# A gated hybrid layer: six of its products done as seven half-sized block products each, in a stage of their own

## The chip, the cores and the metric

The kernel runs on one core of one Trainium2 chip. The metric is the time of one execution on the device in microseconds (us); the times are medians of several runs. The profile is one more execution, taken by the hardware profiler, and its span runs from the first instruction to the last. The engines are TensorE (PE, with its weight loads as PEld), VectorE (DVE), ScalarE (ACT), GpSimd (POOL) and SyncE (SP), which here only issues DMAs.

## What is computed

One decoder layer on 2048 tokens of 1024 features, behind 16 learned meta tokens. One wide input projection feeds two branches: attention with a sliding window of 128 tokens (16 heads, 4 key heads), and a matrix memory (mLSTM, 4 heads) that runs over chunks of 64 tokens. Each branch is gated and projected, the two are merged by sigmoid gates, and there is an output projection with a norm and a residual behind it. Cut to what matters here:

```python
u = rmsnorm(h, norm_pre)
(a_q, a_k, a_v, a_z, m_qk, m_v, m_i, m_f, m_o, m_z, g_a, g_m) = split(u @ w_in)
att = swa_sink_branch(rope(a_q), rope(a_k), a_v)
y_a = (att * silu(a_z)) @ w_attn_out
cell = mlstm_cell(silu(conv(m_qk)), m_v, m_i, m_f)
hm = head_layernorm(sigmoid(m_o) * cell)
y_m = (hm * silu(m_z)) @ w_mlstm_out
merged = sigmoid(g_a) * y_a + sigmoid(g_m) * y_m
out = h + rmsnorm(merged @ w_out, norm_post)
```

Six products in it have 2048 by 1024 results and 1024 terms: a_z, m_z, g_m (columns of w_in) and the three with w_attn_out, w_mlstm_out and w_out. In the kernel they are called az, mz, gm, att, hm and out.

## The kernel before

All products are in float32 accuracy from three matmuls: each operand is split into a rounded part (hi) and the rest (lo), and hi by hi, lo by hi and hi by lo are added in PSUM. ScalarE casts hi, VectorE subtracts for lo. A result tile of 128 by 512 takes 8 blocks of 128 terms, 24 matmuls.

The main stage goes through the tokens in two halves of 1024. In each half it follows a plan of blocks (`PLAN`): four groups, each of an attention block A (q, k, v of 4 heads, `token_proj`), a feature block F (one tile each of q and k, two of ga, `feat_proj`), an mLSTM block M (v and o of one head) and a second feature block (two tiles each of az and mz); at the end of the half two feature blocks with gm. `load_w` (line 163) loads and splits the weights of each block ahead of it. `evict_f` (line 721) writes gates to DRAM.

What attention and the mLSTM do per 128 tokens is written as generators (`attn_block`, line 397, `mlstm_chain`, line 563). `slot()` (line 262) is called after every 6 projection matmuls and lets each generator that is due go on by one step; an attention block is started every 12 slots (`ATT_SLOTS`). So their matmuls stand between projection matmuls, and VectorE, ScalarE and GpSimd do the steps between. At an attention block of the plan `drain()` (line 763) has all queued attention blocks started before the next eight come. Results go to DRAM (`att_d`, `hm_d`). Each mLSTM block of 128 tokens loads a row of maxima, `mrep`, by an SP DMA (line 550).

The last stage takes 512 tokens at a time: it loads att_d and the gate az, multiplies and splits, projects (line 929), the same for hm and mz, merges, and then does the output projection (line 951) with norm and residual.

The order of TensorE's instructions is that of the code. On the other engines, and for the DMAs on SP, a scheduler sets the order by priority when the program is built; on the chip each of them takes its instructions strictly in that order.

## Time and profile before

| | us |
|---|---|
| median of 3 runs | 2421.65 |
| lowest, highest | 2418.39, 2426.34 |
| the profiled execution | 2425.9 |
| its span | 2424.2 |

The span is made of engine times, so a row of it is read as: how long an engine was busy in it, and what ended its idle time. "Releaser" is the instruction behind whose end a waiting one could start. Matmuls overlap, so the start of one to the start of the next tells what one costs, not its duration.

### The profile page before, as it was taken

Reading aid. Unit: us, or ns where it says so; the run is one execution under the profiler, and the core shown is the slowest. Engines: PE = TensorE matmul, PEld = TensorE weight load, DVE = VectorE, ACT = ScalarE, POOL = GpSimd, SP = SyncE. Lnnn points to the kernel's source line nnn. Section 1 sums busy time; section 2 is a strip of 40 time slices with the busy share of each in tenths; the row PEclk is TensorE's granted clock in tenths of the full one; section 3 lists DMA queues with packets and bytes.
Section 4 is the critical chain, followed back from the end, with each engine's and each line's share of the span. In section 5 each row is a group of like instructions: output and inputs, shape, how many; then the busy total and the mean of one; then the engine's idle time right before and its main releaser. Section 6 shows DMA issues by size and latency. Waiting matters only on the chain.

```text
span 2424.2 us, 34730 instructions
## 1 busy us (share of the span) xinstructions
PE 2377.3 (98%) x11725; PEld 2017.7 (83%) x11725; DVE 1404.7 (58%) x3309; ACT 1014.7 (42%) x2674; POOL 558.6 (23%) x1151
## 2 busy tenths in 40 slices
...
GB/s 188 51 49 96 92 56 67 70 101 44 97 56 56 89 103 143 48 59 70 90 58 63 72 47 65 74 86 58 70 85 237 230 191 254 175 254 168 236 176 89
DMA packets 176162, 261.38 MB, mean 108 GB/s; under 512 B 18684, under 2 KB 68176, under 8 KB 175984
## 3 DMA queue, kind: packets, MB, share of 16 engines
q1 hardware_dynamic: 175984, 259.17, 33.7%
...
HBM read 200.35 MB, written 58.76 MB: 107 GB/s over the span
## 4 chain that ended last, share of the span: by engine, by line
PE 82%; DMA 6%; DVE 6%; ACT 3%; issue 2%; POOL 1%; SPq 0%; DVEq 0%; POOLq 0%; ACTq 0%
PE pj L714 35%; PE pj L702 22%; PE pj L929 10%; PE pj L951 3%; PE acc L479 3%; DMA wraw<-in_w 3%; PE s L427 3%; DVE wlo L182 2%; PE acc L546 2%; ACT whi L181 1%; PE tr L452 1%; DMA xs<-att_d 1%; DMA zl<-mz_d 1%; PE tr L400 1%; PE tr L546 1%
## 5 line engine op out<-in xcount | busy, mean ns | idle before, releaser
L714 PE MATMUL pj<-un,whi 128*128 128x512 f32 x2560 | 805.1, 396 | 0.0
L702 PE MATMUL pj<-whi,un 128*128 128x512 f32 (+2 forms) x1952 | 604.1, 371 | 0.0
L714 PEld LDWEIGHTS pj<-un,whi 128*128 128x128 f32 x2560 | 467.3, 188 | 88.4
L714 PE MATMUL pj<-un,wlo 128*128 128x512 f32 x1280 | 501.8, 392 | 0.0
L182 DVE TENSOR_TENSOR wlo<-wraw,whi 128x512 fp32r<-128x512 f32 (+2 forms) x480 | 325.5, 702 | 175.4 <-ACT whi L181 172.5
L702 PEld LDWEIGHTS pj<-whi,un 128*128 128x128 f32 x1952 | 361.3, 188 | 37.7 <-issue 1.3
L181 ACT CAST whi<-wraw 128x512 fp32r<-128x512 f32 (+2 forms) x480 | 283.0, 606 | 229.1 <-DMA wraw<-in_w 135.1
L702 PE MATMUL pj<-wlo,un 128*128 128x512 f32 (+2 forms) x976 | 355.9, 365 | 0.0
L929 PE MATMUL pj<-un,whi 128*128 128x512 f32 x1024 | 315.6, 389 | 5.4 <-DVE part L934 5.2
L714 PEld LDWEIGHTS pj<-un,wlo 128*128 128x128 f32 x1280 | 240.8, 188 | 53.3
L929 PEld LDWEIGHTS pj<-un,whi 128*128 128x128 f32 x1024 | 191.9, 188 | 46.6 <-issue 3.2
L929 PE MATMUL pj<-un,wlo 128*128 128x512 f32 x512 | 199.2, 389 | 0.0
L702 PEld LDWEIGHTS pj<-wlo,un 128*128 128x128 f32 x976 | 184.1, 189 | 14.7
L951 PE MATMUL pj<-whi,un 128*128 128x512 f32 x512 | 164.3, 400 | 8.8 <-DVE y L967 8.2
L727 ACT ACTIVATE xs<-pj 128x512 f32<-128x512 f32 x128 | 76.5, 598 | 209.6 <-PE pj L714 200.2
L436 ACT ACTIVATE P<-s,mn 128x144 f32<-128x144 f32 x256 | 95.1, 376 | 152.5 <-DVE mn L434 150.5
L966 POOL TENSOR_TENSOR yss<-yss,mhalf 128x1 f32<-128x1 f32 x16 | 8.8, 549 | 621.3 <-DVE yss L965 621.3
L445 POOL TENSOR_TENSOR Pm<-P,mn 128x64 f32<-128x64 f32 x64 | 38.0, 594 | 443.8 <-DVE mn L441 351.4
L951 PEld LDWEIGHTS pj<-whi,un 128*128 128x128 f32 x512 | 98.8, 193 | 32.0 <-DVE y L967 9.4
L462 POOL TENSOR_SCALAR_AFFINE_SELECT pp<-pc 128x512 fp32r<-128x512 f32 x120 | 84.5, 704 | 175.7 <-ACT pc L457 164.0
L929 PEld LDWEIGHTS pj<-un,wlo 128*128 128x128 f32 x512 | 96.1, 188 | 20.1
L951 PE MATMUL pj<-wlo,un 128*128 128x512 f32 x256 | 101.8, 398 | 0.5 <-DVE wlo L182 0.5
...
## 6 DMA issues: line engine op xcount, KB each, us to landing
wraw<-in_w_all SPq DMA_DIRECT2D x224, 256.0 KB, 3.3
wraw<-in_w SPq DMA_DIRECT2D x192, 256.0 KB, 3.4
...
```

The lines of the kernel that those rows point to most:

```text
L181: S.copy(hi[:, :w], raw[:, :w])
L182: tt(lo[:, :w], raw[:, :w], f(hi)[:, :w], ALU.subtract)
L427: T.matmul(sp[:, pa, c0:272], lhsT=qs[:, pr, pa, :], rhs=ks[:, i, c0:272], start=(i == 0), stop=(i == 1))
L436: S.activation(P[:, 2 * pa + pr], sp[:, pa, 128:272], AF.Exp, bias=mn[:, 2 * pr + pa:2 * pr + pa + 1], scale=-1.0, accum_out=mn[:, 4 + 2 * ...
L462: G.affine_select(pp[:, i], f(pc)[:, i], pattern=[[0, 4], [-1, 128]], compare_op=ALU.is_gt, fill=0.0, base=0, channel_multiplier=1)
L479: T.matmul(acc, lhsT=l, rhs=r.rearrange("p s q -> p (s q)"), start=(i == 0), stop=(i == len(ops) - 1))
L546: T.matmul(out, lhsT=l[:, a], rhs=r[:, b_], start=(start and n == 0), stop=(stop and n == 2))
L702: T.matmul(ps[:, :w], lhsT=us[k][:, a, o:o + 128], rhs=ww[k][:, :w], start=(n == 0), stop=(n == 3 * KT - 1))
L714: T.matmul(ps, lhsT=ww[k][:, 128 * i:128 * i + 128], rhs=us[k][:, a], start=(n == 0), stop=(n == 3 * KT - 1))
L727: S.activation(th, ps, AF.Tanh, scale=0.5)
L929: T.matmul(ps, lhsT=ww[k][:, 128 * i:128 * i + 128], rhs=us[k][:, a], start=(n == 0), stop=(n == 3 * KT - 1))
L951: T.matmul(ps, lhsT=mg[k][:, a, 128 * i:128 * i + 128], rhs=ww[k], start=(n == 0), stop=(n == 3 * KT - 1))
```

## The change

az, mz and gm leave the main stage. They and the three projections with output weights become 12 sets: each matrix for each half of the tokens, a product of 1024 by 1024 by 1024. Both operands are cut in four blocks of 512 by 512, and the product is made of seven block products instead of eight, by sums and differences of blocks (`PRODS`: P1 to P7). A block product is 48 matmuls of 128 by 512, accumulated in four PSUM banks; some are added upon the bank that another left.

The blocks' sums are made where the operands come from. For weights: copies of a block of 1 MB from DRAM to DRAM on SP, and accumulating DMAs on GpSimd (`weight_sums`), a step of them at each block of the plan. For the tokens: the scaled tiles are stored to DRAM in several places (`tokens`) and three sums and more are made by accumulating DMAs (`token_sums`). For the gated att and hm and for the merged sum: on VectorE, as the results come (`operands`).

The plan now has A, F with q and k alone (256 columns), M, and after every second M an F with four tiles of ga. In the place of `drain()` there is a loop that runs slots while too many attention blocks are queued or unfinished. All memory of the main stage is given back ahead of the new stage, which has pools of its own: raw loads in 4 buffers, split operands in 4, one resident operand per product.

```diff
-        fblock([("ga", i), ("q", i), ("k", i), ("ga", i + 4)])
+        fblock([("q", i), ("k", i)])
         th(i)
-        if i < 3:
-            fblock([("az", 2 * i), ("az", 2 * i + 1), ("mz", 2 * i), ("mz", 2 * i + 1)])
-    fblock([("az", 6), ("az", 7), ("mz", 6), ("mz", 7)])
-    fblock([("gm", i) for i in range(4)])
-    fblock([("gm", i) for i in range(4, 8)])
+        if i % 2:
+            fblock([("ga", 2 * i - 2 + j) for j in range(4)])
     return plan
 
 
 PLAN = _plan()
+MATS = ("az", "mz", "gm", "att", "hm", "out")
...
+    es1 = ExitStack()
+    mconst = pool("mconst", 1, None, es1)
+    units = pool("units", 16, None, es1)
...
+    part_d = dram.tile([KT, 128, SEQ], F32, name="part_d")
+    uo_d = [[dram.tile([128, 4, SB], F32, name=f"uo{c}{i}_d") for i in range(8)] for c in range(SEQ // (2 * SB))]
+    gate_d = {n: dram.tile([KT, 128, SEQ], F32, name=f"{n}_d") for n in ("ga", "gm")}
+    sw_d = [[dram.tile([128, 4 * SB], F32, name=f"sw{m}{i}_d") for i in range(4)] for m in range(len(MATS))]
+    op_d = {(n, c): [dram.tile([128, 4, SB], F32, name=f"op_{n}{c}{i}_d") for i in range(7)]
+            for n in ("att", "hm", "mg") for c in range(SEQ // (2 * SB))}
+
+    def token_sums(c):
+        b00, b10, t2, t1, t3, b11, t4, n01 = uo_d[c]
+
+        def add(dst, src):
+            G.dma_start(out=dst, in_=src, accum_op=ALU.add, max_dma_last_dim=4096)
+
+        add(t1, n01)
+        add(t3, n01)
+        add(t2, b00)
+        yield
+        add(t2, n01)
+        yield
+        add(t4, t2)
+        yield
+
+    def weight_sums():
+        for a in range(0, len(MATS), 2):
+            pair = (a, a + 1)
+
+            def cp(dst, src):
+                nc.sync.dma_start(out=dst, in_=src)
+
+            def add(dst, src):
+                G.dma_start(out=dst, in_=src, accum_op=ALU.add, max_dma_last_dim=4096)
+
+            for m in pair:
+                cp(sw_d[m][2], wq[m, 0, 0])
+                cp(sw_d[m][0], wq[m, 1, 1])
+            yield
+            for m in pair:
+                add(sw_d[m][2], wq[m, 0, 1])
+                add(sw_d[m][0], wq[m, 0, 1])
+            yield
+            for m in pair:
+                cp(sw_d[m][1], sw_d[m][2])
+            yield
+            for m in pair:
+                add(sw_d[m][1], wq[m, 1, 1])
+            yield
+            for m in pair:
+                cp(sw_d[m][3], sw_d[m][1])
+            yield
+            for m in pair:
+                add(sw_d[m][3], wq[m, 1, 0])
+            yield
...
+                c_, s_ = divmod(t0 // SB, 2)
+                for i in ((0, 3), (5, 4, 2))[s_] if s_ == k // 4 else (() if s_ else (1,)):
+                    nc.sync.dma_start(out=uo_d[c_][i][:, k % 4], in_=xs)
+                if s_ != k // 4:
+                    neg = stage.tile([128, SB], F32, name="xs")
+                    S.activation(neg, xs, AF.Copy, scale=-1.0)
+                    nc.sync.dma_start(out=uo_d[c_][7 if s_ else 6][:, k % 4], in_=neg)
...
-                if kind == "A":
-                    drain()
+                if c or pi > 1:
+                    next(sums, None)
+                if pi in (4, 6, 8):
+                    if pi == 4:
+                        usums = token_sums(c)
+                    next(usums)
...
+                        while len(queue) > HALF_BLOCKS - 1 - i or done[0] < total - HALF_BLOCKS + i:
+                            slot()
...
-    p2 = pool("p2", 2)
...
-            for nb_ in range(2):
-                wh, wl = load_w(w2, (2 * ph + nb_) * D * SB, SB, p2)
-                for i in range(4):
-                    j = nb_ * 4 + i
-                    th = p2.tile([128, SB], F32, name="tl", bufs=3)
-                    nc.sync.dma_start(out=th, in_=gate_d[gn][j, :, sl])
-                    ps = ps_p.tile([128, SB], F32, name="pj")
-                    n = 0
-                    for k in range(KT):
-                        for a, ww in ((0, wh), (1, wh), (0, wl)):
-                            T.matmul(ps, lhsT=ww[k][:, 128 * i:128 * i + 128], rhs=us[k][:, a],
-                                     start=(n == 0), stop=(n == 3 * KT - 1))
-                            n += 1
...
+    PRODS = (("P1", 0, "w00", "b00"), ("P2", 1, "w10", "b10"), ("P6", 0, "s2", "t2"), ("P5", 1, "s1", "t1"),
+             ("P7", 0, "s3", "t3"), ("P3", 1, "s4", "b11"), ("P4", 0, "w11", "t4"))
+    NP = len(PRODS)
+    NPAIR = SEQ // (2 * SB)
+    post = pool("post", 1)
+    res = pool("res", 1)
+    ring = pool("ring", 1)
+    ps_1 = pool("ps_1", 4, PSUM)
+    ps_0 = pool("ps_0", 4, PSUM)
+    SETS = [(n, c, ("u", c)) for c in range(NPAIR) for n in ("az", "mz", "gm")]
+    SETS += [(n, c, ("w", n)) for n in ("att", "hm", "out") for c in range(NPAIR)]
+    OPD = {"att": "att", "hm": "hm", "out": "mg"}
+    IDX = {"P1": 0, "P2": 1, "P6": 2, "P5": 3, "P7": 4, "P3": 5, "P4": 6}
+
+    def split(pl, nm, src, p, sign=1.0, bufs=None):
+        raw = src.pop(0)
+        op = pl.tile([128, 2, 2, SB], R, name=nm, **({} if bufs is None else {"bufs": bufs}))
+        if sign == 1.0:
+            S.copy(op[:, 0], raw)
+            tt(op[:, 1], raw, f(op)[:, 0], ALU.subtract)
+        else:
+            S.activation(op[:, 0], raw, AF.Copy, scale=sign)
+            stt(op[:, 1], raw, sign, f(op)[:, 0], ALU.mult, ALU.subtract)
+        return op
...
+    N = len(SETS) * NP
+    fetched, ready, resident = {}, {}, {}
+
+    def fetch(n):
+        u, i = divmod(n, NP)
+        nm, c, key = SETS[u]
+        w_src = weight_src(nm, PRODS[i][2])
+        b_src = (uo_d[c] if key[0] == "u" else op_d[OPD[nm], c])[i]
+        srcs = [w_src, b_src] if key[0] == "u" else [b_src, w_src]
+        if u and SETS[u - 1][2] == key:
+            srcs.pop()
+        fetched[n] = []
+        for src in srcs:
+            for p in range(2):
+                raw = ring.tile([128, 2, SB], F32, name="raw", bufs=4)
+                nc.sync.dma_start(out=raw, in_=src[:, 2 * p:2 * p + 2])
+                fetched[n].append(raw)
+
+    def prep(n):
+        u, i = divmod(n, NP)
+        raws = fetched.pop(n)
+        st = [split(ring, "st", raws, p, bufs=4) for p in range(2)]
+        if raws:
+            sign = -1.0 if SETS[u][2][0] == "u" and PRODS[i][0] == "P6" else 1.0
+            resident[i] = [split(res, f"r{i}{p}", raws, p, sign) for p in range(2)]
+        ready[n] = (st, resident[i])
...
+    def operands(on, c, nh, sh, g, b):
+        d = op_d[on, c]
+        if (nh, sh) == (0, 0):
+            store(d[IDX["P1"]][:, g], b)
+        elif (nh, sh) == (1, 1):
+            store(d[IDX["P3"]][:, g], b)
+        elif (nh, sh) == (0, 1):
+            b11, b22 = keep[0, g], keep[1, g]
+            tt(b11, b11, b, ALU.subtract)
+            store(d[IDX["P5"]][:, g], b11)
+            tt(b, b22, b, ALU.subtract)
+            store(d[IDX["P7"]][:, g], b)
+            stt(b22, b11, -1.0, b22, ALU.mult, ALU.subtract)
+            store(d[IDX["P6"]][:, g], b22)
+        else:
+            store(d[IDX["P2"]][:, g], b)
+            t2 = keep[1, g]
+            stt(t2, t2, -1.0, b, ALU.mult, ALU.subtract)
+            store(d[IDX["P4"]][:, g], t2)
...
+        if e is not None:
+            tt(e, bank, e, ALU.add)
+        v = bank if e is None else e
+        if nm == "gm":
+            th = post.tile([128, SB], F32, name="th", bufs=2)
+            S.activation(th, v, AF.Tanh, scale=-0.5 if nh else 0.5)
+            store(gate_d["gm"][j, :, sl], th)
+        elif nm in ("az", "mz"):
+            a = ld((att_d if nm == "az" else hm_d)[j, :, sl])
+            th = post.tile([128, SB], F32, name="th", bufs=2)
+            S.activation(th, v, AF.Tanh, scale=0.5)
+            stt(th, th, -1.0 if nh else 1.0, v, ALU.add, ALU.mult)
+            b = kept(nh, sh, g)
+            if nm == "az":
+                tt(b, a, th, ALU.mult)
+            else:
+                stt(b, a, hn_t[:, j:j + 1], th, ALU.mult, ALU.mult)
+            operands("att" if nm == "az" else "hm", c, nh, sh, g, b)
+        elif nm == "att":
+            th = ld(gate_d["ga"][j, :, sl])
+            b = post.tile([128, SB], F32, name="bt", bufs=2)
+            stt(b, th, 1.0, v, ALU.add, ALU.mult)
+            store(part_d[j, :, sl], b)
...
+    with tc.high_priority(offset=300):
+        for n in range(2):
+            fetch(n)
+        prep(0)
+    for n in range(N):
+        u, i = divmod(n, NP)
+        nm, c, key = SETS[u]
+        name, bset = PRODS[i][0], (PRODS[i][1] + u) % 2
+        if n + 2 < N:
+            fetch(n + 2)
+        if n + 1 < N:
+            with (tc.high_priority(offset=200) if n == 0 else ExitStack()):
+                prep(n + 1)
+        fresh = name in ("P1", "P2", "P5")
+        if name in ("P1", "P2"):
+            banks[bset] = [(ps_1 if bset else ps_0).tile([128, SB], F32, name="x") for _ in range(4)]
+        st, rs_ = ready.pop(n)
+        ow, ob = (st, rs_) if key[0] == "u" else (rs_, st)
+        order_ = [(p, g, kk) for p in range(2) for g in range(4) for kk in range(2)]
+        if n == N - 1:
+            order_ = [(p, g, kk) for g in range(4) for p in range(2) for kk in range(2)]
+        for p, g, kk in order_:
+            for m, (a, b) in enumerate(((0, 0), (0, 1), (1, 0))):
+                if nm == "out":
+                    l, r = ob[p][:, a, kk, 128 * g:128 * g + 128], ow[p][:, b, kk]
+                else:
+                    l, r = ow[p][:, a, kk, 128 * g:128 * g + 128], ob[p][:, b, kk]
+                T.matmul(banks[bset][g], lhsT=l, rhs=r, start=(fresh and p == 0 and kk == 0 and m == 0),
+                         stop=(p == 1 and kk == 1 and m == 2), skip_group_check=True)
+        for g in range(4):
+            bk = banks[bset][g]
+            if name == "P1":
+                e1[g] = etile()
+                S.copy(e1[g], bk)
+            elif name == "P2":
+                quarter(nm, c, 0, 0, g, bk, e1[g])
+            elif name == "P6":
+                e2[g] = etile()
+                S.copy(e2[g], bk)
+            elif name == "P5":
+                e5[g] = etile()
+                S.copy(e5[g], bk)
+            elif name == "P7":
+                quarter(nm, c, 1, 1, g, bk, e5[g])
+            elif name == "P3":
+                quarter(nm, c, 0, 1, g, bk, e2[g])
+            else:
+                quarter(nm, c, 1, 0, g, bk, None)
```

The order of instructions shows it at three places. The names: `sw11` is the second of four weight sums of the second matrix, `in_wq` the weights, `mrep` the row of maxima for an mLSTM block, `wraw` a weight tile, `att_d` and `hm_d` the stores of results; in brackets stand the semaphores that a row waits for, DMASW for an accumulating DMA of GpSimd, DMAHW for a DMA of SP.

SP, in the first mLSTM block of the plan, before:

```order
L550 DMA mrep_1591<-mr_d_102 128x128 [waits DMAHW4_49,DVE_49,Activation_49]
L550 DMA mrep_1702<-mr_d_102 128x128 [waits DMAHW4_49,DVE_49,Activation_49]
L611 DMA hm_d_104<-tho_1475 128x2x128 [waits DMAHW6_49,Activation_49]
L550 DMA mrep_1819<-mr_d_102 128x128 [waits DMAHW5_49,DMAHW7_49,DVE_49,Activation_49]
L486 DMA att_d_103<-ao_1736 128x2x128 [waits DMAHW0_49,DVE_49]
L611 DMA hm_d_104<-tho_1573 128x2x128 [waits DMAHW1_49,Activation_49]
L550 DMA mrep_1896<-mr_d_102 128x128 [waits DMAHW2_49,DMAHW7_49,DVE_49,Activation_49]
L611 DMA hm_d_104<-tho_1679 128x2x128 [waits DMAHW3_49,Activation_49]
L550 DMA mrep_2007<-mr_d_102 128x128 [waits DMAHW2_49,DVE_49,Activation_49]
```

and after:

```order
L185 DMA sw11_d_132<-sw12_d_133 16x16384 [waits DMAHW2_49,DMASW6_49]
L604 DMA mrep_1425<-mr_d_105 128x128 [waits DMAHW7_49,DVE_49,Activation_49]
L226 DMA wraw2_2184<-in_w_all 128x384 [waits DMAHW4_49]
L185 DMA sw03_d_130<-sw01_d_128 16x16384 [waits DMAHW5_49,DMASW0_49]
L604 DMA mrep_1540<-mr_d_105 128x128 [waits DMAHW3_49,DMAHW6_49,DVE_49,Activation_49]
L185 DMA sw20_d_135<-in_wq 16x16384
L539 DMA att_d_106<-ao_1462 128x2x128 [waits DMAHW0_49,DVE_49]
L185 DMA sw13_d_134<-sw11_d_132 16x16384 [waits DMAHW1_49,DMASW3_49]
L185 DMA sw32_d_141<-in_wq 16x16384 [waits DMAHW2_49]
L604 DMA mrep_1617<-mr_d_105 128x128 [waits DMAHW6_49,DVE_49,Activation_49]
L185 DMA sw30_d_139<-in_wq 16x16384 [waits DMAHW4_49]
```

Between the loads of mrep there are now copies of weight blocks, three of which wait for accumulating DMAs. A little later on SP, at the last weight tiles (`wraw`) of the second attention block, after:

```order
L185 DMA sw41_d_144<-sw42_d_145 16x16384 [waits DMAHW6_49,DMASW3_49]
L665 DMA hm_d_107<-tho_1805 128x2x128 [waits DMAHW7_49,Activation_49]
L226 DMA wraw_2190<-in_w_all 128x384 [waits DMAHW0_49,DVE_49]
L604 DMA mrep_3280<-mr_d_105 128x128 [waits DMAHW4_49,DVE_49,Activation_49]
L185 DMA sw51_d_148<-sw52_d_149 16x16384 [waits DMAHW2_49,DMASW7_49]
L539 DMA att_d_106<-ao_2067 128x2x128 [waits DMAHW3_49,DVE_49]
L226 DMA wraw_2196<-in_w_all 128x384
```

Ahead of each of the two tiles there is now a copy that waits for an accumulation. GpSimd, in the first block of q and k, before (`raw` and `halo` are the convolution's borders, `Pm` and `pmb` probabilities of the meta tokens):

```order
L513 MEMSET rawm 128x38
L502 COPY halo_121<-raw 128x3
L498 COPY raw<-halo_125 128x3
L502 COPY halo_125<-raw 128x3
L498 COPY raw<-halo_121 128x3
L445 TENSOR_TENSOR Pm<-P,mn 128x64
L465 AFFINE_SELECT pc<-pc 128x512 x2
L471 TENSOR_TENSOR pmb<-pm,bm 128x512
```

and after (L169 and L188 are accumulating DMAs, of token tiles and of weights):

```order
L169 DMA uo_d<-uo_d 256x1024
L556 COPY halo_209<-raw 128x3
L463 CAST ks<-km_193 128x2x16
L188 DMA sw_d<-in_wq 256x1024
L552 COPY raw<-halo_205 128x3
L169 DMA uo_d<-uo_d 256x1024
L556 COPY halo_205<-raw 128x3
L188 DMA sw_d<-in_wq 256x1024
L498 TENSOR_TENSOR Pm<-P,mn 128x64
L552 COPY raw<-halo_209 128x3
L188 DMA sw_d<-in_wq 256x1024
L556 COPY halo_209<-raw 128x3
```

Accumulating DMAs now stand between the convolution's steps. TensorE at the end of the main stage, before (L714 the last gm tile, L929 the last stage):

```order
L714 MATMUL pj<-un,whi 128x512 x2
L714 MATMUL pj<-un,wlo 128x512
L929 MATMUL pj<-un,whi_19756 128x512 x2
L929 MATMUL pj<-un,wlo_19757 128x512
L929 MATMUL pj<-un,whi_19762 128x512 x2
```

and after (L779 the last ga tile, L453 to L532 the steps of attention blocks, L1156 the new stage):

```order
L480 MATMUL s<-ks,qs 128x272 x4
L532 MATMUL acc<-pmb,vm_200 128x512
L532 MATMUL acc<-pc,vt 128x512 x2
L532 MATMUL acc<-pp,vt 128x512 x2
L480 MATMUL s<-ks,qs 128x272 x4
L505 MATMUL tr<-ident,P 128x128 x4
L507 MATMUL acc<-ident,Pm 64x128
L532 MATMUL acc<-pmb,vm_200 128x512
L532 MATMUL acc<-pc,vt 128x512 x2
L532 MATMUL acc<-pp,vt 128x512 x2
L1156 MATMUL x<-r_16838,st 128x512 x24
L1156 MATMUL x<-r_16841,st 128x512 x24
```

Steps of attention blocks that stood between projections now stand between the last projection and the new stage.

## Rows read from the trace of the kernel before

**Rows 1.** The page, part 1: busy us, share of the span, instructions of each engine.

```profile
PE 2377.3 (98%) x11725; PEld 2017.7 (83%) x11725; DVE 1404.7 (58%) x3309; ACT 1014.7 (42%) x2674; POOL 558.6 (23%) x1151
```

**Rows 2.** Timeline of TensorE: start us, us, engine, line, operation, tiles, count.

```profile
1800.05 0.61 PE L714 MATMUL pj<-un,whi 128*128 128x512 f32 x2
...
1838.81 0.62 PE L714 MATMUL pj<-un,whi 128*128 128x512 f32 x2
...
1872.12 0.62 PE L929 MATMUL pj<-un,whi 128*128 128x512 f32 x2
```

**Rows 3.** Groups by line: count | busy us, mean ns of one | idle before, releasers.

```profile
L714 PE MATMUL pj<-un,whi 128*128 128x512 f32 x2560 | 805.1, 396 | 0.0
...
L182 DVE TENSOR_TENSOR wlo<-wraw,whi 128x512 fp32r<-128x512 f32 (+2 forms) x480 | 325.5, 702 | 175.4 <-ACT whi L181 172.5
...
L436 ACT ACTIVATE P<-s,mn 128x144 f32<-128x144 f32 x256 | 95.1, 376 | 152.5 <-DVE mn L434 150.5 <-PE tr L323 2.0
...
L462 POOL TENSOR_SCALAR_AFFINE_SELECT pp<-pc 128x512 fp32r<-128x512 f32 x120 | 84.5, 704 | 175.7 <-ACT pc L457 164.0 <-DVE pc L458 9.1 <-PE pj L714 0.2
L465 POOL TENSOR_SCALAR_AFFINE_SELECT pc<-pc 128x512 fp32r<-128x512 f32 x128 | 83.8, 677 | 5.9 <-DVE pc L458 5.9
...
L471 POOL TENSOR_TENSOR pmb<-pm,bm 128x512 fp32r<-128x512 f32 x64 | 73.5, 1149 | 0.0
L490 DVE SCALAR_TENSOR_TENSOR xs<-raw,cw,xs 128x512 f32<-128x512 f32 x96 | 71.9, 749 | 28.7 <-ACT xs L501 17.7 <-POOL halo L502 10.4
L433 DVE TENSOR_REDUCE mn<-s 128x2 f32<-128x288 f32 x128 | 58.1, 454 | 2.5
L429 DVE COPY_PREDICATED s<-um,s 128x256 f32<-128x256 int32 x120 | 50.8, 423 | 51.6 <-PE s L427 51.4
...
L447 DVE TENSOR_TENSOR P<-P,mn 128x512 f32<-128x512 f32 x64 | 46.1, 721 | 4.2 <-POOL Pm L445 1.4
...
L457 ACT CAST pc<-tr 128x512 fp32r<-128x512 f32 x64 | 37.5, 587 | 31.6 <-PE tr L452 29.5 <-POOL ropb L252 1.8
```

**Rows 4.** Waits of TensorE in the whole span, the longest total.

```profile
PE tr L609 <- DVE ks L409: 9.4, 8, 1.5
```

**Rows 5.** Stretches: length; busy PE, PEld, DVE, ACT, POOL; PEclk, DMA share, GB/s.

```profile
1116.00:1170.00 54.00, 54.00 (x262) 45.01 (x262) 31.45 (x83) 21.36 (x66) 12.51 (x22) 1.00 0.25 81
1170.00:1205.00 35.00, 35.00 (x203) 34.69 (x203) 8.43 (x20) 9.99 (x33) 13.13 (x33) 1.00 0.19 59
1205.00:1256.00 51.00, 51.00 (x244) 42.34 (x243) 33.55 (x71) 25.58 (x65) 14.88 (x27) 1.00 0.22 74
1256.00:1319.00 63.00, 62.54 (x339) 52.96 (x337) 45.41 (x138) 32.97 (x102) 22.94 (x52) 1.00 0.19 55
1730.00:1872.00 142.00, 142.00 (x651) 117.74 (x651) 53.73 (x115) 44.04 (x103) 14.71 (x22) 1.00 0.43 144
1872.00:2418.00 546.00, 531.33 (x2306) 435.69 (x2304) 320.03 (x518) 184.23 (x337) 8.23 (x15) 0.99 0.63 199
59.00:155.00 96.00, 93.53 (x467) 76.75 (x466) 71.39 (x199) 48.82 (x135) 30.38 (x55) 0.98 0.17 52
...
40.00:60.00 20.00, 13.87 (x77) 12.76 (x76) 11.55 (x26) 11.19 (x31) 12.21 (x28) 0.83 0.51 163
```

**Rows 6.** Timeline at the end: TensorE's last matmul.

```profile
2417.74 0.39 PE L951 MATMUL pj<-whi,un 128*128 128x512 f32 x1
```

**Rows 7.** Waits of SP in the whole span: us in total, times, longest.

```profile
SPq L550 <- DVE dw L576: 206.8, 59, 7.4
```

**Rows 8.** DMA queue: packets, MB, share of 16 engines; issue: KB each, us to landing.

```profile
q1 hardware_dynamic: 175984, 259.17, 33.7%
...
xr<-in_x SPq DMA_DIRECT2D x16, 512.0 KB, 4.9
```

224 lines of the change are left out of this document (112 added, 112 removed).

## The prediction, made before the changed kernel ran

> **What bounds the kernel now.** The page comes first: TensorE is busy 98% of the span, VectorE 58%, ScalarE 42%, GpSimd 23% [rows 1]. A busy TensorE need not be a fast one, so the second view is the timeline of its matmuls: in a stretch that waits for nothing, 171 projection matmuls of 512 columns start in 38.76 us (1800.05 to 1838.81), 0.227 us each [rows 2]; the 396 ns of their group are durations that overlap [rows 3]. Third, the waits: the longest total of TensorE at any one line is 9.4 us [rows 4]. Its own stream of instructions is the bound. Fourth, the busy times by stretch [rows 5], which show what the average hides. A group of four blocks runs from 1116 to 1319: az and mz (to 1170), an attention block (to 1205), q, k and ga (to 1256), an mLSTM block. VectorE is busy 58%, 24%, 66% and 72% in them, and 38% in the gm blocks (1730 to 1872). In the last stage (1872 to 2418) TensorE shows 531 of 546 us.
>
> **What is removed.** By the code a tile of 128 by 512 results takes 24 matmuls, and az, mz, gm and each output projection have 32 tiles: 6 by 768 = 4608, half of them in the main stage, half in the last (where the row counts 2306 in all [rows 5]). Afterwards 12 sets of 7 products of 48 matmuls, 4032, stand in one stage. 576 fewer by 0.227 us is 131 us off the bound, 5.4% of the span. I make the sum by stage. The main stage ends at 1872.1; without its 2304 matmuls (522 us) it would end at 1350. The new last stage is at least 4032 by 0.227, 914 us. After the last matmul some 6 us remain, from 2417.74 to the span's end [rows 6]. 1350 + 914 + 6 = 2270 us, if nothing new waited. The present last stage takes 546 us for 522 of matmuls; these 24 us of stalls are not in the floor and return below.
>
> **The block sums.** This is the largest term. The order shows 24 copies of 1 MB on SP and 29 accumulating DMAs of 1 MB on GpSimd in the first half. The code spreads them over the plan, but they stand nearly in one stretch: from the loads of the first q, k block to those of the second attention block, between the mrep loads that each mLSTM block waits for. SP and GpSimd take their rows in order; that an SP load holds all behind it until an engine has read its buffer shows in 59 waits of mrep loads for VectorE, 207 us in all [rows 7]. Here a copy waits for an accumulation, and an accumulation for a copy. Ahead of the last weight tile of the second attention block stand 22 copies, and one of them waits for the 24th accumulation. All these must be done before that block can go on.
> Their price: no row has a DMA from DRAM to DRAM, or one that adds. The nearest is the whole queue: 259.17 MB took 33.7% of 16 engines, 0.337 by 2424.2 by 1/259.17 = 3.15 us per MB [rows 8]. Copies at that: 22 by 3.15 = 69 us. A load reads once and writes once; an add has two operands and a result, three streams for two, so I take 1.5 times the row, 4.7 us: 24 by 4.7 = 113 us. The bounds are one price (76 us) and two (151 us). The time they have: where the first feature block starts now (59) the new one starts too; it is 22 us of matmuls shorter and the az, mz block behind it is gone, so the second attention block comes near 155. DMA is busy 17% there [rows 5], 80 of 96 us are free; 16 new stores of token tiles in that stretch are 4 MB, 13 us. 67 us are left. 69 + 113 - 67 = 115 us of standstill; at the ends 78 and 153.
> The trace has all transfers on the one queue of SP [rows 8] and can't say whether a second queue adds capacity. The Trainium skill says that it does not (DMA: Bandwidth & Descriptors, section Issuing engines are not separate DMA queues: transfers of all engines run on the same 16 and interleave, and only issue time is saved). By this rule the sum stays as it is; with a capacity of its own for GpSimd's queue the adds would run beside the copies, and the term would be 113 - 67 = 46 us. The same page has 6.15 us for a GpSimd transfer of 1 MB from HBM to SBUF (section Bandwidth); as an estimate from that page the term would be 69 + 148 - 67 = 150 us.
> The second half has 5 such adds, far apart: 3 us. The token stores ahead of the first feature block: 5 us.
>
> **The main stage.** A group's VectorE work, 31 + 8 + 34 + 45 = 118 us of 203 [rows 5], loses the az, mz block's 8 splits and 8 products (16 by 0.7, 11 us); TensorE's 203 lose 192 matmuls, 44 us: 107 of 159. The mLSTM block stays as it is, 72% and no stall. The q, k block becomes full: an attention block costs VectorE 7.6 us and TensorE 3.9 (the az, mz block's 31.4 less 11, and 54 less 43.5, over the 2.7 that run there). Four convolutions of 4 by 749 ns, 8 splits by 702 [rows 3] and 1.3 attention blocks are 28 us of VectorE over 27 of TensorE. Eight such blocks, for the most part carried into the next: 8 us (0 to 25).
> Attention blocks start every 12 slots. Before, 96 slots and more lay between two attention blocks of the plan, enough for eight; now 48 or 80 and the next block's own. Where that is too few, the code runs slots without a projection. The order shows it twice at each second and fourth attention block, 8 times: transposes of P, then their product with V, and no projection between. In between lie a cast of 587 ns, four selections of 704 and 677 and the product pmb of 1149 on GpSimd [rows 3]: 4.5 us, some 5 with the hand-overs, of which TensorE can use little. 8 by 5 is 40; two stand where the second attention block waits for weights anyway, so 30 (10 to 50).
>
> **The handover.** Now TensorE goes from one stage to the next without a gap (1872.12) [rows 2]. Afterwards the last two attention blocks run out with nothing beside them. Each is scores and normalising (4.7 us: 423, 454, 2 by 376 and 721 ns [rows 3], matmuls and small steps between) and transposes, masks and product (6): 2 by 10.7 and 1.4 for the result, 23 us with 3 of matmuls. The new pools lie in the memory that this frees, and the first load stands behind the last store of att_d: 512 KB take 4.9 us to land [rows 8], the next two 3.2 more, cast and subtraction of 1024 columns twice 587 and 702 ns: 10.7. Together 31 us (20 to 45).
>
> **The last stage's stalls.** The present stage loses 24 of 522 us, 4.5%; on 914 that is 41. Some sets are heavier. In az's and mz's VectorE has 60 instructions of 0.69 us and 14 or 28 splits of 1024 columns (1.24 by the length): 76 us where the operands are read anew, as much as a set's 76 us of matmuls. By DMA hm's first set moves 29 MB, 91 us at 3.15, 15 over; az's first of each pair 25 MB, 79 us, 3 over. 41 + 21 = 62 us (20 to 120).
>
> **Sum.** 2270 + 115 + 8 + 8 + 30 + 31 + 62 = 2524 us of span. The profiled execution took 2425.9 us with a span of 2424.2; the median of the three runs is 2421.65, 2.5 below that span. So 2522 us, 4% slower.
>
> **The rivals.**
> Faster: the sums are hidden. The 22 copies and 24 adds then need no more than the 67 free us, 1.5 us per MB, half the price of any row; or what stands behind them isn't needed when I think. For it: DMA is busy only 17% there, and all sources are there early. Against it: the in-order queues. 2524 - 115 = 2409; with gaps at 15, handover at 25 and stalls at 40 it is 2365. It decides at a standstill of about 12 us: below that the kernel is not slower.
> Worse: the adds cost two prices, and each mLSTM block waits in turn for a load, an add and a copy: rounds of 12 us for 8 of its own, 7 by 4 = 28 more, and TensorE's clock falls in the gaps. The trace has such a stretch: from 40 to 60 TensorE was busy 13.87 of 20 us and the granted share was 0.83 [rows 5], partly at 1.2 and partly at 2.4 GHz. The Trainium skill says that the clock is halved after idling (TensorE: Matmul & The Clock Gate, section Part 1: The HAM clock gate); the row agrees. At that share 64 us of matmuls lose 13. 153 + 28 + 13 = 194 in the place of 115: 2603.
> The last stage is the bound: VectorE or the raw loads (four buffers, all refilled in each product of a set that reads both operands) hold every set at hm's 91 us, 1092 in the place of 976: 2640.
>
> **How the numbers follow.** Forecast 0.52, faster rival 0.26, worse 0.14, last stage 0.08. About 0.3%, 7 us, is what a measurement of this kernel can tell from no change. The faster rival's upper end and the forecast's lowest end touch no change: faster 0.24, same 0.05, slower 0.71. The range: the forecast alone reaches from 2440 to 2600 (its bounds, not all at one end); 2365 takes in most of the faster rival, 2620 most of the worse one.
>
> **What would show it.** The sums: TensorE waiting in the first mLSTM block and at the start of the second attention block, DMA near full there, SP waiting for accumulations; wrong if TensorE is 97% busy from 60 to 200. Their price: the time from issue to landing. The gaps: 8 waits of about 5 us for pmb. The handover: gaps of 20 and 10 us between the last ga matmul and the new stage's first. The last stage: its length against 914 us, hm's first set the longest. All is wrong if matmuls of the new stage start more than 0.227 us apart without a wait.

## The result, and the profile after

The changed kernel takes 2672.3 us (median of 4 runs, 2670.2 to 2679.4) beside 2421.5 for the kernel before: a ratio of 1.104, with a 95% interval from 1.101 to 1.107. It is 10% slower where 4% was predicted, and lies above the range. The profiled execution took 2672.1 us with a span of 2669.5, so the sum of 2524 us of span has to find 145.5 us more.

The page's busy times and three rows of its timeline (40 slices of 67 us, in tenths):

```profile
PE 2354.3 (88%) x11149; PEld 1978.8 (74%) x11149; DVE 1584.6 (59%) x3435; ACT 1109.9 (42%) x2721; POOL 571.6 (21%) x1185
...
PE   7655689999899899899998995999999999959697
...
PEclk8877889999899999899998996999999999979798
DMA  7999721221113651112111113777787677877773
```

TensorE has 576 matmuls less than in [rows 1], yet is busy for only 23 us less: the granted clock is 0.93 in the mean and was 0.99. The hole is in slices 2 to 5, where the DMA row reads 9, 9, 9 and 7; further dents are at slice 25 and at 36 and 38, and the clock is low in the same places. The same by stretch (columns as in [rows 5]: us, busy us and count of PE, PEld, DVE, ACT and POOL, granted clock, DMA share, GB/s):

```profile
104.00:160.00 56.00, 28.68 (x110) 22.24 (x111) 19.44 (x48) 11.47 (x32) 11.89 (x20) 0.73 1.03 244
160.00:210.00 50.00, 27.17 (x128) 21.32 (x126) 13.69 (x46) 9.09 (x31) 13.66 (x26) 0.82 1.02 235
210.00:260.00 50.00, 22.62 (x81) 17.79 (x82) 12.30 (x41) 9.17 (x31) 9.71 (x19) 0.67 1.03 256
...
1326.00:1460.00 134.00, 121.05 (x638) 106.03 (x637) 85.21 (x255) 61.74 (x209) 54.68 (x119) 0.94 0.14 42
...
1610.00:1651.00 41.00, 13.14 (x42) 8.98 (x40) 13.79 (x33) 11.60 (x33) 8.44 (x12) 0.57 0.28 93
...
2351.00:2405.00 54.00, 26.05 (x85) 19.25 (x84) 29.86 (x43) 6.45 (x8) 0.00 (x0) 0.68 0.76 237
...
2650.00:2669.50 19.50, 0.31 (x2) 0.00 (x0) 9.99 (x15) 0.69 (x2) 1.01 (x2) 0.58 0.76 257
```

From 104 to 363 stand the first mLSTM block and the second attention block; up to 260 the DMA engines are full and TensorE works half the time. The pair at 1326 is the same kind of pair late in the second half, with DMA at 14%: 134 us, a clock of 0.94; the first pair takes 259 us. 1610 to 1651 is the handover from the main stage to the new one, 2351 to 2405 the stretch after hm's first set, and behind 2650 stands what follows the last matmul. TensorE's waits (us in total, times, longest):

```profile
PE x L1156 <- DVE ld L1122: 49.0, 8, 15.7
PE s L480 <- ACT ks L461: 36.9, 19, 2.7
...
PE pj L767 <- DVE wlo L232: 18.7, 7, 3.9
PE tr L505 <- DVE P L500: 16.9, 10, 4.3
...
PE x L1156 <- DMA raw<-uo_d: 12.3, 1, 12.3
PE s L480 <- ACT P L489: 9.2, 4, 6.5
...
PE acc L532 <- POOL pmb L524: 5.4, 6, 4.1
```

Before, the longest total was 9.4 us [rows 4]. L1122 is the product with the gm gate in an hm eviction (the instructions that empty a set's PSUM banks), ks the split keys of an attention block, wlo the lo part of a weight tile, P the probabilities (L489 the exponentials, L500 their scaling), pmb the tile that the prediction had named for the gaps.

The queues from 56 to 360, and SP's and GpSimd's longest waits there:

```profile
q0 software_dynamic: 7888, 30.41, 53.7%
q1 hardware_dynamic: 12253, 36.22, 34.5%
...
sw_d<-in_wq POOLq DMA_DIRECT2D x24, 1024.0 KB, 19.2
```

```profile
SPq L185 <- DMA sw_d<-in_wq: 94.5, 9, 19.1
```

```profile
POOL sw_d L188 <- DMA sw_d<-sw_d: 67.8, 10, 14.8
```

The 29 accumulating DMAs on q0 took 53.7% of 304 us, 163 us or 5.6 each; 4.7 were assumed. Copies (SP) wait for adds (94.5 us in 9 waits) and adds (GpSimd) for copies (67.8 in 10), as the order had shown.

### The profile page after: what moved, and what is told of

Its sections match the earlier page's. It is cut to its first block, busy times and chain, and to the rows that moved or that the text cites. A ratio compares the mean times of both kernels' runs of the same rounds, so it can differ in the third digit from the quotient of the medians.

```text
span 2669.5 us, 34039 instructions
## 1 busy us (share of the span) xinstructions
PE 2354.3 (88%) x11149; PEld 1978.8 (74%) x11149; DVE 1584.6 (59%) x3435; ACT 1109.9 (42%) x2721; POOL 571.6 (21%) x1185
## 5 line engine op out<-in xcount | busy, mean ns | idle before, releaser
L1156 PE MATMUL x<-r,st 128*128 128x512 f32 x2688 | 626.4, 395 | 46.1 <-DVE ld L1122 21.0
L767 PE MATMUL pj<-whi,un 128*128 128x512 f32 (+2 forms) x1952 | 633.7, 385 | 0.0
L1156 PEld LDWEIGHTS x<-r,st 128*128 128x128 f32 x2688 | 512.8, 191 | 159.9 <-DVE ld L1122 14.7
L767 PEld LDWEIGHTS pj<-whi,un 128*128 128x128 f32 x1952 | 382.4, 198 | 41.6 <-issue 1.7
L767 PE MATMUL pj<-wlo,un 128*128 128x512 f32 (+2 forms) x976 | 371.1, 380 | 18.7 <-DVE wlo L232 18.7
L1156 PE MATMUL x<-st,r 128*128 128x512 f32 x1344 | 311.9, 395 | 28.0 <-DVE ld L1122 28.0
L779 PE MATMUL pj<-un,whi 128*128 128x512 f32 x1024 | 326.9, 401 | 0.0
L1156 PEld LDWEIGHTS x<-st,r 128*128 128x128 f32 x1344 | 255.8, 191 | 83.9 <-issue 16.1
L978 DVE TENSOR_TENSOR st<-raw,st 128x1024 fp32r<-128x1024 f32 x168 | 205.0, 1222 | 173.1 <-ACT st L977 168.9
L977 ACT CAST st<-raw 128x1024 fp32r<-128x1024 f32 x168 | 176.5, 1052 | 271.5 <-PE x L1156 201.3
L767 PEld LDWEIGHTS pj<-wlo,un 128*128 128x128 f32 x976 | 193.5, 198 | 39.4 <-DVE wlo L232 22.1
L779 PEld LDWEIGHTS pj<-un,whi 128*128 128x128 f32 x1024 | 188.7, 191 | 35.0
L779 PE MATMUL pj<-un,wlo 128*128 128x512 f32 x512 | 202.8, 396 | 0.0
L489 ACT ACTIVATE P<-s,mn 128x144 f32<-128x144 f32 x256 | 95.4, 379 | 143.5 <-DVE mn L487 141.4
L480 PE MATMUL s<-ks,qs 128*128 128x272 f32 (+1 forms) x512 | 101.2, 318 | 55.0 <-ACT ks L461 36.9
L779 PEld LDWEIGHTS pj<-un,wlo 128*128 128x128 f32 x512 | 97.8, 191 | 21.7
## 6 DMA issues: line engine op xcount, KB each, us to landing
sw_d<-in_wq POOLq DMA_DIRECT2D x24, 1024.0 KB, 19.2
```

Of the source, the lines that this page charges most:

```text
L480: T.matmul(sp[:, pa, c0:272], lhsT=qs[:, pr, pa, :], rhs=ks[:, i, c0:272], start=(i == 0), stop=(i == 1))
L489: S.activation(P[:, 2 * pa + pr], sp[:, pa, 128:272], AF.Exp, bias=mn[:, 2 * pr + pa:2 * pr + pa + 1], scale=-1.0, accum_out=mn[:, 4 + 2 * ...
L767: T.matmul(ps[:, :w], lhsT=us[k][:, a, o:o + 128], rhs=ww[k][:, :w], start=(n == 0), stop=(n == 3 * KT - 1))
L779: T.matmul(ps, lhsT=ww[k][:, 128 * i:128 * i + 128], rhs=us[k][:, a], start=(n == 0), stop=(n == 3 * KT - 1))
L977: S.copy(op[:, 0], raw)
L978: tt(op[:, 1], raw, f(op)[:, 0], ALU.subtract)
```

## Where the 145 us are: parts left out one by one

Four kernels take parts away. Each was run once, beside the kernel before, which took 2422 to 2426 us; so differences of less than some 7 us say little. The first, no_wsum, leaves out the weight sums:

```diff
-        sums = weight_sums()
+        sums = iter(())
...
-        v = sw_d[m][int(name[1]) - 1] if name[0] == "s" else wq[m, int(name[1]), int(name[2])]
+        v = wq[m, 0, 1] if name[0] == "s" else wq[m, int(name[1]), int(name[2])]
```

> The 24 copies and 24 accumulating DMAs of the weight sums are left out; the last stage reads a plain weight block in the place of each sum (same loads). The changed kernel profiles at a span of 2669.5 us; its first mLSTM and second attention block together take 259 us, the later pairs 135 to 140. Theory (the weight sums fill the DMA engines and hold the in-order queues of SP and GpSimd): this stretch falls to about 140, span 2520 to 2550, and what stood still before the first q, k block (15 us) goes in part. Rival (token sums, the VectorE load of the q, k block or slots without projections cause the standstill): it falls by less than 40 us, span above 2630.

The span is 2555.2 us, 114.3 less; the first pair of blocks takes 148 us. That is a little above the theory's figures and far from the rival's, and the prediction had 115 for this term. But 131 us above the kernel before are then left without any weight sum.

bare leaves out the token sums too (stores, negated tiles and adds).

> Neither weight sums nor token sums (their stores, negations and adds) are made; the last stage reads plain blocks in their place. Without the weight sums alone the span is 2555.2 us and the main stage ends at 1498.5, 148 us above its matmuls' 1350. Theory (sums are apart from the rest, the token sums worth 32 as on spread sums): main stage to 1460 to 1472, span 2517 to 2530, so that some 115 us above the matmuls are left that have nothing to do with sums. Rival (the two hide one another: the gaps are late work of the sums): span below 2500.

2518.5 us, 36.7 less, inside the theory's range. On the spread kernel (below) the same removal gave 31.6:

> The spread kernel without the token sums: the stores and negations of token tiles and their 10 accumulating DMAs are left out, and the last stage reads plain token tiles in their place. Around the start of the second half the trace of the changed kernel has an ga block of 62 us (others 53), an attention block of 50 (others 39 to 41) and a q, k block of 27 to 35 (others 25), DMA 60 to 70% busy; the first q, k block starts 8.5 us after its weights' block ends. Theory (the stores, and GpSimd behind the adds, cost this): 20 to 35 us less, span 2528 to 2544, the attention block down to about 42. Rival (it is the raw loads and splits of the second half's tokens, and would be there without the stores): less than 8 us.

2531.8, as the theory had it; the attention block at the second half's start fell from 46 to 41 us.

bare_att8 also starts attention blocks every 8 slots:

```diff
-ATT_SLOTS = 3 * SLOTS
+ATT_SLOTS = 2 * SLOTS
```

> As bare, with attention blocks every 8 slots. Theory (what is left above the matmuls is slots without projections and the clock that falls in them): main stage 40 to 60 us shorter than in bare, handover from 40 to 12, span 2430 to 2455. Rival (it is VectorE, fuller since a pair of blocks has the same work in less of TensorE's time): main stage less than 25 us shorter, span above 2465.

2422.0 us, 96.5 less and better than the theory's best. With this one number changed, the kernel without sums is level with the kernel before. The main stage, the handover and the last stage of bare, and then of bare_att8, by stretch:

```profile
58.00:1466.00 1408.00, 1319.12 (x6820) 1131.77 (x6819) 901.44 (x2524) 657.63 (x2036) 495.90 (x1056) 0.96 0.19 57
1466.00:1506.00 40.00, 12.22 (x39) 8.30 (x37) 13.54 (x33) 10.74 (x30) 8.47 (x12) 0.56 0.30 94
1506.00:2498.00 992.00, 934.70 (x4032) 766.14 (x4032) 605.95 (x781) 392.95 (x538) 9.07 (x14) 0.96 0.75 239
```

```profile
61.00:1404.00 1343.00, 1291.22 (x6855) 1112.88 (x6854) 904.91 (x2553) 668.59 (x2061) 502.72 (x1068) 0.99 0.20 61
1404.00:1418.00 14.00, 0.83 (x4) 0.40 (x2) 4.93 (x5) 5.85 (x7) 0.00 (x0) 0.67 0.87 295
1418.00:2403.00 985.00, 932.21 (x4032) 765.59 (x4031) 603.93 (x780) 390.58 (x537) 9.92 (x15) 0.96 0.75 240
```

The main stage ends 61 us earlier (its last projection at 1404.5, not 1465.5), the handover falls from 40 to 13. TensorE's waits in the main stage add up to 88 us in bare and to 52 in bare_att8, 37 less (14 in the kernel before). The other 24 of the 61 are left by difference, and the granted clock, 0.96 and 0.99, is what else differs. The 37 are a net figure: the waits for ks and for P at L500 fall from 44 us to 2 and those for wlo from 17.5 to nothing, but the waits for the exponentials (L489) rise from 5.9 to 35.1. How a gap costs twice is seen in the trace without weight sums. In each row: start, duration, instruction, and in brackets the idle time before it:

```profile
1319.21 0.34 PE L767 MATMUL pj<-whi,un 128*128 128x384 f32 x1
1320.89 0.66 PE L505 MATMUL tr<-ident,P 128*128 128x128 f32 x4 [1.34 <-DVE P L500]
1321.39 0.27 PE L507 MATMUL acc<-ident,Pm 128*64 128x128 f32 x1
1321.49 0.49 PE L453 MATMUL tr<-ident,qkv 128*128 128x128 f32 x3
1324.39 1.37 PE L480 MATMUL s<-ks,qs 128*128 128x272 f32 x4 [2.41 <-ACT ks L461]
1325.94 0.80 PE L532 MATMUL acc<-pmb,vm 128*128 128x512 f32 x1 [0.18 <-POOL pmb L524]
```

Between the projections (L767) stand all parts of two attention blocks with nothing beside them: slots that the code runs without a projection. TensorE waits 1.3 us for P and 2.4 for the next block's keys; when pmb is wanted it is nearly there (0.18 us). The same trace in steps of 6 us around it:

```profile
1317.00:1323.00 6.00, 3.65 (x24) 3.08 (x22) 3.09 (x10) 2.89 (x12) 2.64 (x6) 0.99 0.08 23
1323.00:1329.00 6.00, 4.43 (x12) 3.59 (x13) 2.66 (x8) 0.84 (x3) 3.02 (x5) 0.50 0.01 1
1329.00:1335.00 6.00, 4.78 (x27) 4.46 (x25) 2.96 (x9) 2.38 (x13) 0.50 (x1) 0.94 0.07 22
1335.00:1341.00 6.00, 2.88 (x14) 2.15 (x15) 3.65 (x11) 1.67 (x5) 5.16 (x11) 0.91 0.01 3
```

The clock is at 1.2 GHz (0.50) behind two waits of which none is over 2.5 us, in the stretch where the four score matmuls take 1.37 us and not 0.67. With blocks 8 slots apart, the pair at 1134 in bare_att8, the peer of the one at 1326 above:

```profile
1134.00:1250.00 116.00, 112.87 (x636) 100.53 (x637) 83.23 (x251) 58.99 (x201) 53.52 (x117) 1.00 0.16 46
```

636 matmuls in the place of 638, 116 us in the place of 134.

bare_nopart is bare without the second load of each hm eviction:

```diff
-            th, pt = ld(gate_d["gm"][j, :, sl]), ld(part_d[j, :, sl])
+            th = ld(gate_d["gm"][j, :, sl])
+            pt = th
```

> As bare, with the loads of part_d in the hm sets left out (64 of 128 KB partitions' width, 8 MB; the gate tile stands in for it). In the changed kernel six products around the hm sets take 17 to 30 us in the place of 10.9, TensorE waiting for the product behind the gm load; VectorE waits for part_d there. Theory (two loads per tile in three buffers, behind stores on SP: the latency of part_d): last stage 990 to 1000 in bare, 935 to 955 here. Rival (operand transfers make these stretches long): less than 15 us of difference.

2464.1 us, 54.4 less than bare; the last stage takes 938.7 us and not 992.3:

```profile
1506.00:2445.00 939.00, 923.13 (x4032) 759.80 (x4032) 603.25 (x782) 393.63 (x539) 10.04 (x15) 0.99 0.75 244
```

The load is 8 of 237 MB there, and the DMA share is 0.75 as in bare, so it is not the volume. The trace of the changed kernel shows VectorE as it empties hm's banks (start, duration, idle time before):

```profile
2385.24 0.69 DVE L1124 SCALAR_TENSOR_TENSOR bt<-ld 128x512 f32<-128x512 f32 x1 [4.68 <-DMA ld<-part_d]
2385.97 0.69 DVE L1056 SCALAR_TENSOR_TENSOR b<-b,bt 128x512 f32<-128x512 f32 x1
2386.58 0.68 DVE L1122 SCALAR_TENSOR_TENSOR ld<-ld,x 128x512 f32<-128x512 f32 x1
2391.33 0.69 DVE L1124 SCALAR_TENSOR_TENSOR bt<-ld 128x512 f32<-128x512 f32 x1 [4.07 <-DMA ld<-part_d]
```

2 us of work and 4 of waiting for a load per tile. Three buffers hold one tile and a half, so a load goes out only when a buffer comes free. TensorE waits at the first two products of the next set (26.8 and 30.0 us in the place of 10.9), whose banks are not empty yet. That it is the buffers alone was not shown: with five of them (ld5, below) the stage took 33 us less, not 54.

By the ends of the main stage and the spans, the terms are:

| term (us) | predicted | measured | from |
|---|---|---|---|
| weight sums, main stage | 115 | 112 | its end at 1610.1, 1498.5 without |
| token stores and sums | 8 | 33 | 1498.5 to 1465.5 |
| slots without projections (blocks 12 slots apart, not 8) | 30 | 61 | 1465.5 to 1404.5 |
| the rest above 1350 | 8 | 54 | 1404.5 less 1350 |
| handover | 31 | 40.5 | 1610.1 to 1650.6 |
| last stage above 914 | 62 | 86 | 999.7 less 914 |
| behind the last matmul | 6 | 19 | 2650.3 to 2669.5 |

The differences add up to 145 us. The figures belong to this order of removal: with the weight sums spread and the token sums in place, the 8 slots gave 70 us of span (s_att8, below) and not 96.5. And last stages with the same instructions, in other kernels, took 985.0 to 999.7 us, so that its row is good to some 10 us.

## What a sum costs, and where

plain makes the 24 adds of weights copies that don't add, on the same queue with the same waits.

```diff
-                G.dma_start(out=dst, in_=src, accum_op=ALU.add, max_dma_last_dim=4096)
+                G.dma_start(out=dst, in_=src, max_dma_last_dim=4096)
```

> Same DMAs, same queues, same waits, but the 24 weight DMAs of GpSimd copy and do not add. In the trace of the changed kernel GpSimd's queue takes 53.7% of 304 us for 29 MB (5.6 us each), SP's 34.5% for 36 MB (2.9 per MB). Theory (an accumulating DMA costs nearly two copies, and the sums are bound by DMA time): 24 by 2.7, some 65 us of DMA time less, span 2595 to 2625. Rival one (it is GpSimd's queue that is dear, not the adding): its price stays at 5 us and more, span within 15 us of 2669. Rival two (the chain copy, add, copy is bound by waiting and not by DMA time): price falls, span within 20 us of 2669.

2635.4 us, 34 less, between the cases. The queues from 56 to 325:

```profile
q0 software_dynamic: 7888, 30.41, 39.4%
```

39.4% of 269 us is 106; less five token sums at 5.6 (taken as before) it leaves 3.2 us for each of the 24 copies. So the dear part is the adding, 1.7 times a copy on the same queue (1.5 assumed), and the pair falls from 259 to 217 us: 42 of its 111 us are the adding, 69 the rest. Both rivals are wrong as they stand, but the span fell by 34 where the queue's time fell by 57 (163 to 106), as it would if part of the standstill is the chain's waiting; that part was not measured by itself.

The Trainium skill says that a second issuing engine adds no capacity (DMA: Bandwidth & Descriptors, section Issuing engines are not separate DMA queues). The trace agrees: with both queues at work the share stands at 1.02 and 1.03.

spread keeps every sum and moves the weight sums: each of their DMAs is queued behind the last instruction of its engine that the code wrote before it.

```diff
+            def behind(engine):
+                return tc.issue_after(next(i for i in reversed(nc.cur_bb.bb.instructions) if i.engine == engine))
...
+                with behind(mybir.EngineType.SP):
+                    nc.sync.dma_start(out=dst, in_=src)
...
+                with behind(mybir.EngineType.Pool):
+                    G.dma_start(out=dst, in_=src, accum_op=ALU.add, max_dma_last_dim=4096)
```

> The same copies and adds, each queued behind the last instruction of its engine that the code wrote before it, so that a step stands in its own block of the plan (18 steps, from the third block to about two thirds of the main stage) and not all in the first 300 us. Theory (the loss comes from all of it meeting in one stretch with full DMA engines, which are 20% busy later): nearly all of the standstill goes, span 2525 to 2565. Rival (every add holds the load queue wherever it stands, 48 transfers of 3 to 6 us): it is only moved, span above 2620.

2563.4 us, 106.1 less and 8 more than without the sums. The main stage ends 16 us later than without them (1514.8 and 1498.5); the last stage is 8 us shorter, which is within what such stages differ by. From 56 to 1300 the queue shows

```profile
q0 software_dynamic: 9248, 35.65, 15.2%
```

for 34 adds: 15.2% of 1244 us, 5.6 each, the same price, with the DMA engines less than half busy:

```profile
95.00:249.00 154.00, 129.93 (x688) 113.60 (x689) 91.30 (x274) 65.00 (x216) 59.54 (x130) 0.90 0.46 115
249.00:1250.00 1001.00, 924.38 (x4708) 787.97 (x4707) 617.48 (x1689) 460.09 (x1406) 355.38 (x744) 0.96 0.41 117
```

What cost 112 us of main stage in one place costs 16 when it is spread.

best3 is the opposite test, with all weight sums in the second half, on a kernel that is told of below:

> As best (span 2435.6, attention blocks every 8 slots, spread sums, five load buffers), with the weight sums all in the second half, the three pairs of matrices three plan blocks apart, so that two steps that stand in one block are of different matrices. In best the second half's pairs take 116 and 118 us, as in bare_att8 (118 and 116), though a third of the weight sums stands there; the first half's take 133 and 130 against 126 and 126, and its q, k blocks 38 and 32 against 25. Theory (sums cost where DMA and the load queue have no room, and the second half has room): 15 to 35 us less than best, span 2400 to 2420, faster than the kernel before by up to 1%. Rival (sums cost as much wherever they stand, two steps to a block more so): span 2430 or more.

The rival was right: 2472.3 us, a ratio to the kernel before of 1.022 (1.019 to 1.024). The first half's pairs fell to 125 and 124, but the second half's first pair rose from 116 to 125, 17 us stood between a q, k and an mLSTM block (4 in best), and an attention block took 47 us and not 34. The last stage was 10 us longer too, which is within what such stages differ by. Room on the average (a DMA share of 0.51 there) was not enough. That it is the two steps to a block was not tried apart; the token sums of the second half stand in the same blocks.

## Other trials

ld5 gives the part_d tile the two buffers that the tanh leaves idle in hm sets, so five buffers stand for three:

```diff
-            th, pt = ld(gate_d["gm"][j, :, sl]), ld(part_d[j, :, sl])
+            th = ld(gate_d["gm"][j, :, sl])
+            pt = post.tile([128, SB], F32, name="th", bufs=2)
+            nc.sync.dma_start(out=pt, in_=part_d[j, :, sl])
```

> In the evictions of the hm sets the part_d tile is loaded to a buffer pair of its own (the one of the tanh, idle in these sets), so five buffers serve what three served (two loads per tile). The trace shows TensorE waiting 49 us for the product behind the gm load in the hm sets, at clocks of 0.68 and 0.73 there, and VectorE waiting for part_d. Theory (too few load buffers make each eviction wait for a fresh load): these waits fall under 15 us, the last stage from 1000 to about 950, span 2610 to 2630. Rival (the loads are late because the DMA engines are 76 to 83% busy with operands): less than 15 us, span above 2655.

2645.0 us, 24.5 less, between the cases; the last stage takes 966.8, 33 less, while the main stage, in which nothing was changed, ends 9 later. Of the 49 us of waits there are left

```profile
PE x L1158 <- DVE ld L1124: 18.7, 5, 5.7
```

s_ldst is spread with these five buffers and with GpSimd as the issuer of the last stage's stores:

> The spread kernel with five load buffers in the hm sets (as ld5) and the last stage's stores issued by GpSimd, which is idle there, in the place of SP. In ld5 24 us of the waits remained; SP waits there for VectorE's results in stores, with the next loads behind them. Theory (SP's order, loads behind stores that wait, makes the evictions late): last stage from 990 to 925 to 945, span 2495 to 2520. Rival (the transfers themselves are the bound, and GpSimd's queue is dearer, 5.6 against 2.9 us per MB): last stage 965 or longer, span above 2538.

2578.5 us, 15 more than spread. The last stage takes 999.8: longer than ld5's 966.8 with the same buffers, and no shorter than spread's 989.5 with three. The hm wait is gone, but TensorE now waits for operands:

```profile
PE x L1163 <- DVE st L983: 30.1, 5, 8.6
```

The rival's side came true; that GpSimd's queue is dearer for plain stores was not measured by itself. best_hp asked for earlier loads in another way, by priority:

> As best, with the loads of the last stage's evictions (att_d, hm_d, ga, gm, part_d, x) given 60 instructions of priority, so that SP issues them as soon as a buffer is free and ahead of stores that wait for VectorE. Theory (in the last stage it is SP's order and not the transfers that makes loads late): 10 to 30 us less than best. Rival (the transfers' time, DMA 76 to 90% busy in the hm sets, is the bound): within 6 us of best, or longer, since operand loads then come later.

2441.6 us of span beside 2435.6 of best (told of below), no difference in the medians (2444.3 and 2441.6), the rival again: the waits move from the hm product (18.9 us to 0.6) to operands (13 to 32).

s_att8 is the 8-slot spacing on the spread kernel:

> The spread kernel (span 2563.4 us), with one attention block started every 8 slots in the place of 12. With the weight sums left out the main stage still took 148 us more than its matmuls; its trace shows TensorE waiting 36 us for the split of k (ks), 17 for Pm and 9 for P, at clocks of 0.92 to 0.95 in each mLSTM and attention pair (134 to 149 us each, four of them), where the code runs slots without a projection; then 27 us of run-out at the main stage's end. Theory (too few slots for blocks 12 apart cause the gaps, and the gaps the lower clock): pairs of 110 to 120, run-out under 12, span 2460 to 2495. Rival (VectorE, 84 to 87% busy in the mLSTM blocks, can't go faster: the waits come back under other names): pairs above 128, span above 2535.

2493.7 us, 70 less, near the theory's end. The second half's pairs fell to 117 and 116, the first half's only to 144 and 130 (126 in bare_att8), and its last ga block and the next q, k block took 73 and 56 (69 and 26 in bare_att8). There one sees what an add in GpSimd's order does (GpSimd, then VectorE):

```profile
825.68 0.20 POOL L468 CAST ks<-km 128x32 fp32r<-128x32 f32 x1
855.56 0.89 POOL L169 DMA_DIRECT2D uo_d<-uo_d  x1 [29.68 <-DMA uo_d<-uo_d]
856.15 0.49 POOL L557 COPY raw<-halo 128x3 f32<-128x3 f32 x1
```

```profile
856.67 2.98 DVE L549 SCALAR_TENSOR_TENSOR xs<-raw,cw,xs 128x512 f32<-128x512 f32 x1 [24.95 <-POOL raw L557]
```

An add waits 30 us for an earlier one on the same destination, behind it stands the copy of three columns that the convolution needs, and TensorE stood for 27 us. s_tok therefore queues the token sums' adds apart:

> The spread kernel, with the token sums' accumulating DMAs too queued behind the last GpSimd instruction written before them, so that the three steps stand two blocks of the plan apart. In the trace of the kernel with blocks every 8 slots GpSimd waits 29.7 us for one accumulation upon the same destination (uo_d), the convolution's copies are behind it, VectorE's convolution waits 25 us for these and TensorE 27; the first half has 12 us of waits for Pm behind such adds. Theory (dependent adds in GpSimd's order hold the convolution; of the 31.6 us that leaving out the token sums gave, most is this): 12 to 28 us less, span 2535 to 2552. Rival (the 31.6 us are the stores' transfers and the negations): less than 8 us, span above 2555.

2560.3 us, only 3 less and none of it in the main stage: with 12 slots this wait was not on the path (1.4 us of it in spread's trace), and the rival's number came out. best has spread sums, these adds apart, 8 slots and five buffers:

> All that gained so far: spread weight sums, spread token sums, attention blocks every 8 slots, five load buffers in the hm sets. Against the 2493.7 us of the third alone on spread sums: 25 to 40 less for the token sums (27 us of TensorE's waits at the second half's start, 12 in the first), 20 to 33 less for the buffers: span 2420 to 2450, no faster than the kernel before (2424.2). If the gains hide one another: above 2455.

The span is 2435.6; 2441.6 us in the median, a ratio of 1.008 (1.005 to 1.011) to the kernel before. It takes back nearly all of the loss and is still slower, by less than 1%. Its main stage ends 22 us before that of s_att8 (1448.2 and 1470.3); the buffers act in the last stage alone, so with 8 slots the adds' place did count. It ends 44 us behind bare_att8's (1404.5): that is what all the sums still cost. s_all, with the stores on GpSimd and without the adds apart, came to 2502.0: above what was expected, and near what its parts had measured by then (2563.4 less 70 and 15 more). The number is the one given for VectorE as the new bound, but the parts account for it without that:

> Spread sums, attention blocks every 8 slots, five load buffers and stores on GpSimd together. If the losses are apart and add up: 2563 less 70 to 100 (gaps and run-out) less 45 to 65 (last stage): span 2400 to 2450, about the kernel before (2424.2). If VectorE takes over as the bound in the main stage: above 2480.

In best TensorE waits most for exponentials, so best2 gave this step one slot more; it also began the weight sums two plan blocks later:

```diff
-ATT_YIELDS = (3, 3, 5, 5)
+ATT_YIELDS = (3, 4, 5, 4)
...
-                if c or pi > 1:
+                if c or pi > 3:
```

> As best (span 2435.6), with one slot moved inside an attention block (3, 4, 5, 4 slots between its parts in the place of 3, 3, 5, 5), since TensorE waits 37 us there for the exponentials of the first pair of heads before it may write the second pair's scores, and with the weight sums begun two plan blocks later. Theory (each of these waits is short of about one slot, 1.4 us, in 17 places; the first half loses some 60 us to the second, part of it to the sums): 10 to 25 us less, span 2411 to 2426, level with the kernel before. Rival (VectorE is behind in these blocks and the wait only moves to the product with V): within 6 us of best.

A miss on both sides, 2464.6 us. The two rows are best's longest wait and best2's:

```profile
PE s L486 <- ACT P L495: 37.0, 17, 7.5
```

```profile
PE tr L669 <- DVE ks L468: 28.9, 20, 1.6
```

The wait for P fell to 5.4 us, and the mLSTM's transposes (L669) now wait 20 times for the split of keys; the second half's pairs rose from 116 and 118 to 126 and 125. As two things were changed at once, and the last stage, left as it was, took 10 us more, how the 29 us divide stays open.

## Why the prediction went wrong, step by step

**The direction and the floor were right.** Matmuls of the last stage start 0.227 us apart where nothing waits (48 in 10.9 us), so 2270 us stands as what the matmuls need.

**The block sums were right in place and size**, 112 us of main stage for 115. The place was argued from the order, and the first stretch shows all four marks that the prediction named: waits in the first mLSTM block and the second attention block, DMA at 1.03, SP waiting 94.5 us for adds, and 19.2 us from issue to landing. The size is in part luck: the adds cost 5.6 us and not 4.7, and five token adds in the same stretch had not been priced. With these the prediction's own sum would have come to 164 us (69 + 29 by 5.6 - 67); what hid the other 52 was not told apart.

**The token stores and sums, 8 us, were 33.** The prediction took 5 us for the stores ahead of the first feature block and 3 for the second half's adds, with no row behind either. It left out the second half's stores, the negations on ScalarE and what stands behind the adds on GpSimd. By place (no_wsum less bare) 7 us stand ahead of the first mLSTM block, 12 in the first pair and 13 in the first two blocks of the second half. How they divide by cause was not told apart, but for the adds' place: with 12 slots, moving them gave nothing in the main stage (s_tok).

**The gaps and the q, k block were the step that failed most:** 30 + 8 us were taken, and 115 were left above 1350 without any sum (bare). That slots without a projection appear was right, read from the order. Their price was not: "two stand where the second attention block waits for weights anyway, so 30" took one wait per place, for pmb, and pmb's waits are 5.4 us in all. The waits are for ks (19 times, 36.9 us) and P, since two attention blocks run against each other there; in bare's main stage these two alone are 44 us. And it left out the clock, which the prediction had only in the rival "worse": with blocks 8 slots apart 24 of the 61 us are left for it, by difference.

For the q, k block the prediction had compared VectorE's sum with TensorE's, and expected that what is left over is carried into the next block. The changed kernel shows this: all but 0.2 of the 18.7 us of waits for wlo stand in mLSTM blocks right behind a q, k block. That is more than 8 and within the bounds. The row of 54 us in the table is not this term alone. In bare_att8, without sums and with the gaps closed, 52 us of waits are left in the main stage, the most of them for the exponentials of attention blocks:

```profile
PE s L480 <- ACT P L489: 35.1, 17, 7.4
```

In the changed kernel this wait is 9.2 us, so most of it comes with the 8 slots. The three longest gaps of the second half stand right behind q, k blocks, where the convolutions are still on VectorE: a step that is due after three slots is late well before the engine is full. How the 115 us divide between the spacing, VectorE and the clock was not shown beyond this.

**The handover, 31 us, was 40.5:** 28 of run-out (23 had been reckoned, matmuls included), and 12.3 for the first load (10.7). bare_att8 shows its condition: with 8 slots 13 us are left.

**The last stage, 62 us, was 86.** The price of hm's first set was taken from its bytes, 15 us. The bytes were not what counted: the second load of each tile, in three buffers, was, 54 us over both hm sets. The place was right, though the wait shows in the products of the set behind (111 us; hm's first set itself took 76). The 32 us that are left (25 in bare_nopart) are below the 41 that had been taken in proportion.

**The end, 6 us, was 19.** Behind the last matmul VectorE still has nine products with loads of x, which come one by one through the same three buffers:

```profile
2657.84 0.75 DVE L1068 SCALAR_TENSOR_TENSOR b<-b,yss,ld 128x512 f32<-128x512 f32 x1 [2.50 <-DMA ld<-in_x]
...
2662.85 0.75 DVE L1068 SCALAR_TENSOR_TENSOR bt<-bt,yss,ld 128x512 f32<-128x512 f32 x1 [1.60 <-DMA ld<-in_x]
```

The prediction took this end over from [rows 6], a property of a stage that the change replaces.

**Of the rivals**, "faster" falls twice. Where the sums were nearly hidden (spread) the kernel was 5.7% slower than the kernel before, so the standstill of 12 us at which it was to decide was wrong too: it stood on the other terms. "Worse" had the right extra mechanism, the clock: it fell in the stretch of the sums (0.67 to 0.82) as this rival said, but also in gaps all through the main stage, and the sums came to 112 us where it had 194. The last stage as the bound of every set did not come: 75 of its 84 products take 10.9 or 11.0 us.
